# Moving one 32-byte tile: the address phase of matmul operands in a two-layer block

## The chip, the cores and the metric

The kernel runs on one core of one Trainium2 chip. The metric is device time in microseconds (us) of one launch; the median of three runs is 1803.8 us (1799.57, 1803.80 and 1804.04). A profiled execution shows every instruction of the five engines (PE is TensorE, DVE is VectorE, ACT is ScalarE, POOL is GpSimd, SP is SyncE) and its DMA packets. PE has a second row, PEld, for the loading of weights: a matmul streams one operand (the moving one, here up to 512 columns) past another that was loaded before (the stationary one, 128 columns).

## The reference, cut to what matters

Two layers act on 256 tokens of width 2048, in float32. Each layer normalizes, applies a scale and a shift that depend on a conditioning vector, widens to 4096, mixes, and projects back. Layer 0 mixes with a Fourier transform and also works on 256 context tokens; layer 1 is windowed attention over tokens and context.

```python
h = _rmsnorm(x, norm_g[i]) * (1 + scale) + shift
if kind == 0:
    y  = _fourier_branch(h, fnet_w_in[j], fnet_w_mix[j])
    yc = _fourier_branch(hc, fnet_w_in[j], fnet_w_mix[j])
elif kind == 1:
    y, yc = _attention_branch(h, hc, attn_w_in[j], attn_sink[j], rows, cols, need_ctx)
x = x + gate * (y @ w_out[i])
...
return _rmsnorm(x, final_g)
```

## The kernel before

A float32 product is made of three matmuls on a pair of halves: each operand is split into a high part (`h`, a rounded copy of type float32r) and a low part (`l`, the rest). `mm3` (L77 to L80) issues the three: `wh` with `xh` on L78, `wh` with `xl` on L79, `wl` with `xh` on L80. In a row such as `ps<-act,wh` the first name behind the arrow is the moving operand and the second the stationary one. Weights come in pieces of 1 MB through the pool `raw`, and ACT (L65) and DVE (L66) split them into tiles `wh` and `wl` of the pool `ws`, 1024 columns each.

The stages in the order of time, with the lines that the prediction names:

- Layer 0, opening and Fourier groups, to 322 us: matmuls of 256 or 260 columns.
- Layer 0, gate product and output product, 322 to 1022 us: `mm3` with 512 columns. The moving operand is a tile of the pool `act` (the activations, both parts), the stationary one a slice of `wh` or `wl`.
- Layer 1, keys and values, 1022 to 1120 us: `mm3` with 512 columns. Here the weights move, and slices of the normalized input are stationary: `h` (tokens, 16 tiles of the pool `h1`) and `h1c` (context, pool `kvp`).
- Layer 1, attention, 1160 to 1640 us: 64 heads, and between the steps of one head come units of other products as filling: queries (`mm3`, weights moving, `h` stationary), gate (L1119 with 512 columns and L1121 with 256: `h` moves, a slice of `wh` or `wl` is stationary), and the first part of the output product. Of a head itself are L1155 and L1156 (scores: `kkh` and `kkl` move, `qa` or `qb` is stationary), the softmax on ACT (L1160, L1172) and DVE (L1157, L1173), a transpose of its result `f` into `ft` by DMA (L1175), and L1190 and L1191 (16-bit products of `ft` with the values `v`).
- Layer 1, output product, to 1787 us: `mm3` with 512 columns, weights moving and slices of the gated result stationary. That result has 32 blocks `k`; `y_split` (L976) puts blocks 0 to 15 into the pool `h1` (its slots are free by then), 16 to 23 into the pool `act`, and 24 to 31 into the pool `fin`. The tiles are called `ys` in the rows, those of `act` `act`.
- The last sums, the normalization and the stores, to 1800 us.

The order of the instructions on each engine is set by the program and a scheduler that runs when the program is built. Pools take their room in the order in which they are opened, one behind the other, each tile rounded up to 32 bytes. So the byte at which a tile begins in a partition follows from all that was opened before it. The pools `raw`, `ws` and `act` are opened early. The pool `h1` of layer 1 is opened after them and began with a 32-byte tile `dsc`, which holds one scale per key-value head (written in `d_turn`, read in `emit_y` at L1140):

```python
with tc.tile_pool(name="h1", reuse_waits="tile", bufs=16) as h1p:
    hx1 = []
    v01, vs = [], []
    dsc = h1p.tile([P, 8], F32, name="dsc", bufs=1)
```

Of the kernel before, what the change touches and what calls it, by code (L numbers as in the profile page):

```python
# [10 lines left out]
F32 = mybir.dt.float32  # L11
# [6 lines left out]
P = 128  # L18
# [13 lines left out]
def tile_dit(ctx: ExitStack, tc: tile.TileContext, a: dict, out: bass.AP):  # L32
    nc = tc.nc
    V, S, PE, GP = nc.vector, nc.scalar, nc.tensor, nc.gpsimd

    const = ctx.enter_context(tc.tile_pool(name="const", bufs=1))
# [40 lines left out]
    def mm3(o, wh, wl, xh, xl, start, stop):  # L77
        PE.matmul(o, wh, xh, start=start, stop=False)  # L78
        PE.matmul(o, wh, xl, start=False, stop=False)  # L79
        return PE.matmul(o, wl, xh, start=False, stop=stop).ins  # L80
# [18 lines left out]

    ident = const.tile([P, P], F32, name="ident")  # L100
    make_identity(nc, ident)
    ones = const.tile([P, 1], F32, name="ones")
    GP.memset(ones, 1.0)
    mhalf, pow_end = const.tile([P, 4], F32, name="mhalf"), [None]
    GP.memset(mhalf, -0.5)

    def bcast_rows(r4, dst):
        o = psum()
        for t in range(4):
            PE.matmul(o[:, t * P : (t + 1) * P], r4[:, t : t + 1].broadcast_to([P, P]), ident, start=True, stop=True)  # L110
        S.copy(dst, o)
# [54 lines left out]
    with tc.tile_pool(name="st", reuse_waits="tile", bufs=1, side="right") as st:  # L166
# [3 lines left out]
        ss = st.tile([P, 4], F32, name="ss")  # L170
# [716 lines left out]
    with tc.tile_pool(name="h1", reuse_waits="tile", bufs=16) as h1p:  # L887
        hx1 = []
        v01, vs = [], []
        dsc = h1p.tile([P, 8], F32, name="dsc", bufs=1)  # L890
        kT = []
        with tc.tile_pool(name="kvp", reuse_waits="tile", bufs=2) as kvp:
            hc1 = []
# [70 lines left out]
        with tc.tile_pool(name="at", reuse_waits="tile", bufs=2) as at:  # L964
# [4 lines left out]
            def w1_next():  # L969
                n = kg1[0]  # L970
                kg1[0] += 1
                if n % 2 == 0:
                    raw1[0] = raw(a["wo1a"][n // 2])
                return half_split(raw1[0], n % 2)

            def y_split(k):  # L976
                if 16 <= k < 24:
                    t = act(F32R)
                else:
                    t = (h1p if k < 16 else fin[0]).tile([P, 512], F32R, tag="h1" if k < 16 else "ys", name="ys", bufs=16)  # L980
                split(t[:, 0:N], t[:, N : 2 * N], y1[k // 2][:, (k % 2) * N : (k % 2 + 1) * N], GP if k < 24 else V)
                yh.append(t)

            def o1_step(k, os_, wh, wl):
                while len(yh) <= min(k + 4, NB - 1) and (len(yh) < 24 or fin):
                    y_split(len(yh))
                for tb in range(2):
                    mm3(os_[tb], yh[k][:, tb * P : (tb + 1) * P], yh[k][:, N + tb * P : N + (tb + 1) * P], wh, wl, k == 0, k == NB - 1)
# [251 lines left out]
        with tc.tile_pool(name="fin", reuse_waits="tile", bufs=1) as fp:  # L1240
# [7 lines left out]
                    nc.gpsimd.dma_start(x2[tb][c], x1d[tb, :, c * 512 : (c + 1) * 512])  # L1248
            fg = fp.tile([P, D], F32, name="fg")
            nc.gpsimd.dma_start(fg, a["fg"].broadcast_to([P, D]))  # L1250
            ss = fp.tile([P, 9], F32, name="ss")

            sum_end = [None]

            def evac(tb, cb, o, c0=0, c1=512, col=None, square=True):
                col = tb * 4 + cb if col is None else col
                q, qx = slice(cb * 512 + c0, cb * 512 + c1), slice(c0, c1)
                t, x = act()[:, 0 : c1 - c0], x2[tb][cb][:, qx]
                V.tensor_tensor(t, o[:, qx], gbc[:, q], op=ALU.mult)
                sum_end[0] = V.tensor_tensor(x, x, t, op=ALU.add).ins  # L1260
                if square:
                    S.activation(t, x, AF.Square, accum_out=ss[:, col : col + 1])
                if cb < 3:
                    GP.tensor_tensor(x, x, fg[:, q], op=ALU.mult)

            for k in range(24, NB, 2):
                w = w1_next()
                for i in range(2):
                    o1_step(k + i, oA, *(t[:, i * 512 : (i + 1) * 512] for t in w))
            for tb in range(2):  # L1270
                evac(tb, 0, oA[tb])
            o = [[psum() for _ in range(2)] for _ in range(2)]
# [182 lines left out]
```

## Time and profile before

| | before |
|---|---|
| median of three runs | 1803.8 us |
| span of the profiled execution | 1799.6 us (the lowest of the three runs, 1799.57, to the digit shown) |
| PE busy | 1765.1 us, 98% |
| DVE, ACT, POOL busy | 1411.3, 898.3, 213.5 us |
| instructions | 26039 |
| granted TensorE clock, mean | 0.998 |
| transfers | 398.86 MB, mean 222 GB/s |

A row of the profile's groups has the line, the engine, the operation, the tiles and their shape, the count, the busy time in us, the mean ns of one, and behind the second bar the idle time of the engine just before them. [...]

### The profile page before, as it was taken

To read this page: it belongs to the slowest core of one execution; us is meant where nothing else is said; L and a number is where in the kernel's file an instruction comes from. 1 tells how busy PE (TensorE), PEld (TensorE's weight loads), DVE (VectorE), ACT (ScalarE), POOL (GpSimd) and SP (SyncE) were. 2 spreads that over 40 slices of the span, in tenths; PEclk is the share of its full clock that TensorE was granted. 3 is DMA by queue.
4 is the path that set the end of the run, shared out by engine and by line. 5 is a ranking of instruction groups with operands and counts; after the bars stand their busy time and mean duration, and the time that the engine had idled before them with its cause. 6 is when DMAs were issued, how large, how long until landed. Compare 5 with 4: busy or idle time off the path is not lost. (4 is left out here: it accounts for less than half of the span.)

```text
span 1799.6 us, 26039 instructions
## 1 busy us (share of the span) xinstructions
PE 1765.1 (98%) x9449; PEld 1478.0 (82%) x9449; DVE 1411.3 (78%) x2761; ACT 898.3 (50%) x1543; POOL 213.5 (12%) x213
## 2 busy tenths in 40 slices
PE   6999999999999999999999999999999999999998
PEld 4679999888888888888888888878888788887886
DVE  5779888786978888775976563989999899997455
ACT  5545445432222242323322443678887788886343
POOL 0001112100000000000001000332212212233001
PEclk9999999999999999999999999999999999999999
DMA  9998889666666757663558322488888988888553
GB/s 393 417 341 230 236 228 249 230 227 241 239 229 234 260 194 264 245 223 117 189 203 336 120 104 94 168 189 217 213 209 204 211 209 209 211 211 263 192 176 140
DMA packets 205248, 398.86 MB, mean 222 GB/s; under 512 B 152064, under 2 KB 152464, under 8 KB 170048
## 3 DMA queue, kind: packets, MB, share of 16 engines
q1 hardware_dynamic: 181056, 359.19, 61.7%
q0 software_dynamic: 19920, 31.06, 6.7%
q10 hardware_dynamic: 4144, 6.95, 1.2%
q8 instruction: 74, 1.21, 0.3%
q14 instruction: 54, 0.44, 0.1%
HBM read 352.06 MB, written 12.59 MB: 203 GB/s over the span
## 5 line engine op out<-in xcount | busy, mean ns | idle before, releaser
L65 ACT CAST wh<-raw 128x1024 fp32r<-128x1024 f32 x333 | 348.3, 1048 | 532.4 <-PE ps L79 431.6
L66 DVE TENSOR_TENSOR wl<-raw,wh 128x1024 fp32r<-128x1024 f32 x333 | 428.0, 1289 | 219.1 <-ACT wh L65 215.4
L79 PE MATMUL ps<-act,wh 128*128 128x512 f32 x1024 | 398.2, 389 | 0.0
L78 PE MATMUL ps<-act,wh 128*128 128x512 f32 x1024 | 393.7, 389 | 0.0
L80 PE MATMUL ps<-act,wl 128*128 128x512 f32 x1024 | 392.8, 389 | 0.0
L80 PEld LDWEIGHTS ps<-act,wl 128*128 128x128 f32 x1024 | 192.2, 188 | 39.9
L79 PEld LDWEIGHTS ps<-act,wh 128*128 128x128 f32 x1024 | 192.2, 188 | 39.8
L78 PEld LDWEIGHTS ps<-act,wh 128*128 128x128 f32 x1024 | 192.2, 188 | 39.7
L1119 PE MATMUL ps<-h,wh 128*128 128x512 f32 x512 | 184.8, 396 | 0.0
L686 DVE CUSTOM_DVE_ANT_0 raw<-raw,cb 128x512 f32<-128x512 f32 x256 | 172.7, 689 | 12.7 <-DMA raw<-in_adw 8.9
L686 DVE CUSTOM_DVE_ANT_0 junk<-raw,cb 128x512 f32<-128x512 f32 x192 | 132.1, 688 | 31.0 <-DMA raw<-in_adw 20.4
L1121 PE MATMUL ps<-h,wl 128*128 128x256 f32 x512 | 138.6, 281 | 0.0
L79 PE MATMUL ps<-wl,h 128*128 128x512 f32 x320 | 126.9, 397 | 0.3 <-DVE wl L66 0.3
L80 PE MATMUL ps<-wh,h 128*128 128x512 f32 x320 | 125.3, 395 | 0.0
L78 PE MATMUL ps<-wh,h 128*128 128x512 f32 x320 | 124.0, 402 | 0.0
L1173 DVE SCALAR_TENSOR_TENSOR f<-p,sm,f 128x512 f16<-128x512 f32 x128 | 105.6, 844 | 11.1 <-ACT f L1172 10.9
L1119 PEld LDWEIGHTS ps<-h,wh 128*128 128x128 f32 x512 | 96.2, 188 | 18.9
L1160 ACT ACTIVATE p<-ps,mx 128x512 f32<-128x512 f32 x128 | 88.0, 689 | 36.9 <-DVE mx L1157 30.8
L1172 ACT ACTIVATE f<-p,sm 128x512 f16<-128x512 f32 x128 | 87.6, 717 | 33.6 <-DMA ft<-f 15.5
L1121 PEld LDWEIGHTS ps<-h,wl 128*128 128x128 f32 x512 | 96.6, 189 | 2.8
L1157 DVE CUSTOM_DVE_ANT_0 ps<-ps,mask,nsink 128x512 f32<-128x512 f32 x128 | 93.5, 750 | 0.9 <-PE ps L1156 0.7
L79 PE MATMUL ps<-wl,ys 128*128 128x512 f32 (+1 forms) x192 | 75.2, 392 | 0.0
(339 smaller groups left out, 3379.3 us busy)
## 6 DMA issues: line engine op xcount, KB each, us to landing
raw<-in_wz SPq DMA_DIRECT2D x64, 1024.0 KB, 5.4
raw<-in_adw SPq DMA_DIRECT2D x64, 1024.0 KB, 5.2
raw<-in_awp SPq DMA_DIRECT2D x32, 1024.0 KB, 13.0
raw<-in_wo SPq DMA_DIRECT2D x32, 1024.0 KB, 5.5
raw<-in_wq SPq DMA_DIRECT2D x32, 1024.0 KB, 5.3
raw<-in_wu SPq DMA_DIRECT2D x32, 1016.0 KB, 6.1
raw<-in_wo1b SPq DMA_DIRECT2D x16, 1024.0 KB, 4.9
act<-in_xT POOLq DMA_DIRECT2D x32, 256.0 KB, 6.0
```

What stands on the lines that cost most here:

```text
L65: last_cast[0] = S.copy(h, src).ins
L66: last_sub[0] = eng.tensor_tensor(l, src, h.bitcast(F32), op=ALU.subtract).ins
L78: PE.matmul(o, wh, xh, start=start, stop=False)
L79: PE.matmul(o, wh, xl, start=False, stop=False)
L80: return PE.matmul(o, wl, xh, start=False, stop=stop).ins
L686: V.tensor_tensor_reduce(junk if s == 0 and i < 3 else wf, wf, cb[:, s, kq * 512 : kq * 512 + 512], 1.0, 0.0, ALU.mult, ALU.add, acc[:, i, ...
L1119: PE.matmul(o[0], wh[:, q], hx1[k], start=k == 0, stop=k == KT - 1)
L1121: PE.matmul(o[0][:, 0:N], wl[:, q], hx1[k][:, 0:N], start=False, stop=False)
L1157: V.tensor_tensor_reduce(o, o, mask[:, tb, :], -0.125, nsink[:, i : i + 1], ALU.add, ALU.min, mx[:, tb : tb + 1])
L1160: S.activation(pt[tb], so[tb], AF.Exp, bias=mx[:, tb : tb + 1], scale=-1.0, accum_out=sm[:, tb : tb + 1])
L1172: S.activation(f[:, 0:512], pt[tb], AF.Copy, scale=sm[:, tb : tb + 1])
L1173: V.scalar_tensor_tensor(f[:, 512:1024], pt[tb], sm[:, tb : tb + 1], f[:, 0:512], op0=ALU.mult, op1=ALU.subtract)
```

## The change

The two constants `ones` (4 bytes in a partition) and `mhalf` (16 bytes) each took 32 bytes of the pool `const`. They become slices of one tile `consts` of 32 bytes: columns 0 to 3 hold -0.5, columns 4 to 7 hold 1.0. In the 32 bytes so freed stands `dsc`, which leaves the pool `h1`. The pool `const` keeps its length, so nothing that is opened between the two moves; all that is opened from `h1` on begins 32 bytes lower. Besides, the 36-byte tile `ss` of the last stage is taken after blocks 24 to 31 of `ys` in the pool `fin` and not before them.

```diff
@@ constants
-    ones = const.tile([P, 1], F32, name="ones")
-    GP.memset(ones, 1.0)
-    mhalf, pow_end = const.tile([P, 4], F32, name="mhalf"), [None]
+    consts = const.tile([P, 8], F32, name="consts")
+    ones, mhalf, pow_end = consts[:, 4:5], consts[:, 0:4], [None]
+    GP.memset(consts[:, 4:8], 1.0)
     GP.memset(mhalf, -0.5)
+    dsc = const.tile([P, 8], F32, name="dsc")
@@ layer 1
     with tc.tile_pool(name="h1", reuse_waits="tile", bufs=16) as h1p:
         hx1 = []
         v01, vs = [], []
-        dsc = h1p.tile([P, 8], F32, name="dsc", bufs=1)
         kT = []
@@ last stage
             nc.gpsimd.dma_start(fg, a["fg"].broadcast_to([P, D]))
-            ss = fp.tile([P, 9], F32, name="ss")
-
             sum_end = [None]
...
                 for i in range(2):
                     o1_step(k + i, oA, *(t[:, i * 512 : (i + 1) * 512] for t in w))
+            ss = fp.tile([P, 9], F32, name="ss")
             for tb in range(2):
                 evac(tb, 0, oA[tb])
```

In the built program the instructions of every engine stand in the same order as before, with the same shapes and the same waits; only start addresses differ. The start of a tile in its partition, modulo 256 bytes (slices of 128 float32 columns keep it, being 512 bytes apart):

| tiles | role in layer 1 | before | now |
|---|---|---|---|
| `wh`, `wl`, `act`, `v` (pools `ws`, `act`) | moving, stationary | 224 | 224 |
| `h` (and `ys`, blocks 0 to 15) | stationary, moving | 0 | 224 |
| `h1c` | stationary | 0 | 224 |
| `kkh`, `kkl` | moving | 0 | 224 |
| `qa`, `qb` | stationary | 0 | 224 |
| `ys`, blocks 24 to 31 | stationary | 64 | 224 |
| `p`, `gbc`, `fg` | not of a matmul | 0 | 224 |
| `f`, `ft` (in and out of the DMA transposes; `ft` moves in L1190, L1191) | moving | 192 | 160 |

The tiles `raw`, `ws` and `act` lie in the lower part of a partition (bytes 19,680 to 136,416), those that the change shifts above it (from byte 142,048 on). In layer 0's Fourier groups, whose tiles don't move, some operands of 256 and 260 columns stay at other values than 224.

## The prediction

> **What bounds the kernel now.** I read the page first, then the busy times by stage, then the chain of waits with the matmuls' starts.
>
> ```profile
> span 1799.6 us, 26039 instructions
> PE 1765.1 (98%) x9449; PEld 1478.0 (82%) x9449; DVE 1411.3 (78%) x2761; ACT 898.3 (50%) x1543; POOL 213.5 (12%) x213
> ```
>
> PE is busy all the time; the question is whether it is the bound in layer 1, the only part whose addresses move. The table of stretches (columns: stretch, time, then busy time and count of PE, PEld, DVE, ACT, POOL, the granted clock, the DMA engines' share, GB/s) answers:
>
> ```profile
> 400.00:800.00 400.00, 400.00 (x1767) 331.20 (x1766) 325.26 (x766) 114.28 (x137) 5.88 (x11) 1.00 0.65 238
> 1040.00:1100.00 60.00, 60.00 (x259) 48.31 (x258) 30.42 (x54) 19.25 (x31) 0.00 (x0) 1.00 0.27 95
> 1022.00:1120.00 98.00, 97.81 (x447) 79.69 (x447) 52.18 (x99) 41.95 (x72) 1.58 (x2) 1.00 0.34 119
> 1172.00:1600.00 428.00, 423.92 (x2346) 353.39 (x2347) 398.74 (x738) 348.30 (x689) 100.65 (x73) 1.00 0.86 208
> 1650.00:1787.00 137.00, 137.00 (x592) 110.90 (x591) 73.87 (x74) 55.41 (x67) 12.61 (x8) 1.00 0.50 175
> ```
>
> In keys and values and in the output product PE has no gap, and the next engine (DVE) is busy 53% and 54%: there a nanosecond less for a matmul is a nanosecond of the end. In attention PE is busy 99%, but DVE 93% (398.74 of 428) and the DMA engines 86%: PE still sets the pace, with little room before another does. The clock is granted in full throughout.
>
> What does a 512-column matmul cost? 400 to 800 us (layer 0, both operands at 224) holds 1767, of which some two reach over the edges: 400.0/1765 = 226.6 ns from start to start. 1040 to 1100 us (layer 1, weights at 224 moving, `h` or `h1c` at 0 stationary): 60.0/257 = 233.5 ns. Same clock, same shape, no gap: 6.9 ns more. The chain of waits shows it best, in one stage with one line of code and the same moving tiles (columns: start, duration, what; one row per block `k`, which is 4 times the three matmuls of `mm3`):
>
> ```profile
> 1657.08 0.93 PE ps L78 x4
> ...
> 1699.08 0.93 PE ps L78 x4
> ...
> 1701.88 0.91 PE ps L78 x4
> 1704.60 0.91 PE ps L78 x4
> 1707.32 0.91 PE ps L78 x4
> ...
> 1720.92 0.91 PE ps L78 x4
> 1723.64 0.94 PE ps L78 x4
> ...
> 1726.45 0.94 PE ps L78 x4
> ...
> 1729.26 0.94 PE ps L78 x4
> ```
>
> Blocks 0 to 15 (`ys` at 0): 16 steps from 1657.08 to 1701.88, 2.80 us each, 233.3 ns a matmul. Blocks 16 to 23 (the same data in `act`, at 224): 8 steps to 1723.64, 2.72 us, 226.7 ns. Block 24 on (`ys` at 64): 5.62 us for two, 234.2 ns. Nothing but the place of the stationary operand changes at these two borders. The groups say the same by duration (mean ns behind the busy time):
>
> ```profile
> L79 PE MATMUL ps<-act,wh 128*128 128x512 f32 x1024 | 398.2, 389 | 0.0
> L79 PE MATMUL ps<-wl,h 128*128 128x512 f32 x320 | 126.9, 397 | 0.3 <-DVE wl L66 0.3
> L79 PE MATMUL ps<-wl,ys 128*128 128x512 f32 x184 | 73.0, 397 | 0.0
> L79 PE MATMUL ps<-wl,act 128*128 128x512 f32 x56 | 21.8, 390 | 0.0
> ```
>
> **The change, part by part.** It removes and adds no instruction and no wait; two memsets of `ones` and `mhalf` become two of one tile, at the start. All that can act is where operands begin. I take it that equal phase (224 for both) costs 226.7 ns wherever the tile lies.
>
> (a) Matmuls with 512 columns, weights moving. By the three lines of `mm3`: `h` 3 × 320 = 960, `h1c` 3 × 64 = 192, `ys` 3 × 184 = 552, and 12 with both moving `act` and stationary `ys`: 1716. At 2.80 − 2.72 us over 12 matmuls, 6.67 ns each: 11.4 us. Of them 3 × 192 = 576 lie between 1172 and 1600 us: 3.8 us in attention, 7.6 us outside.
>
> (b) The scores, where both operands stand at 0, and (c) the gate's pair L1119 and L1121. The timeline of PE:
>
> ```profile
> 1501.02 0.40 PE L1155 MATMUL ps<-kkh,qa 128*128 128x512 f32 x1
> 1501.26 0.39 PE L1156 MATMUL ps<-kkl,qa 128*128 128x512 f32 x1
> 1501.48 0.39 PE L1155 MATMUL ps<-kkh,qa 128*128 128x512 f32 x1
> 1501.71 0.40 PE L1156 MATMUL ps<-kkl,qa 128*128 128x512 f32 x1
> 1501.95 0.40 PE L1119 MATMUL ps<-h,wh 128*128 128x512 f32 x1
> ...
> 1502.30 0.39 PE L1119 MATMUL ps<-h,wh 128*128 128x512 f32 x1
> 1502.53 0.28 PE L1121 MATMUL ps<-h,wl 128*128 128x256 f32 x1
> ...
> 1504.38 0.39 PE L1119 MATMUL ps<-h,wh 128*128 128x512 f32 x1
> ```
>
> Four score matmuls take 0.93 us, 232.5 ns each, though both stand at 0; but inside (0.24, 0.22, 0.23, 0.24) the slow steps are those at the border to another product, and the step from `kkl` to the next `kkh` takes 0.22. So equal phase is quick here too, in the upper part of the partition, and the border costs. At 226.7 ns: 5.8 × 256 = 1.5 us; bounds 0 and that. The gate's pairs: six in 2.08 us, 0.347 each, about 0.23 for the 512 columns (`h` at 0 moving) and 0.12 for the 256. I put 3 ns on the first and nothing on the second, since the 256-column row shows no quicker kind: 3 × 512 = 1.5 us. Bounds: nothing, and the whole pair by the ratio 2.72/2.80, 10 ns × 512 = 5.1 us.
>
> (d) L1190 and L1191: `ft` stood at 192 against `v` at 224 and now stands at 160. Unequal before and after, so nothing; if the 2.9% of (a) were lost or won on two times 256 matmuls of about 0.11 us, 1.6 us either way:
>
> ```profile
> 1497.46 0.27 PE L1191 MATMUL ps<-ft,v 128*128 128x256 f16 x1
> 1497.57 0.27 PE L1190 MATMUL ps<-ft,v 128*128 128x256 f16 x1
> 1497.68 0.27 PE L1191 MATMUL ps<-ft,v 128*128 128x256 f16 x1
> ```
>
> (e) The other engines write and read shifted tiles too. The same cast into `ys` (0 and 64) and into `act` (224) costs the same, so nothing:
>
> ```profile
> L65 ACT CAST ys<-act 128x256 fp32r<-128x256 f32 x24 | 8.2, 403 | 0.7 <-DVE act L1140 0.7
> L65 ACT CAST act<-act 128x256 fp32r<-128x256 f32 x8 | 2.6, 399 | 0.0
> ```
>
> Sum: 7.6 outside attention, and 3.8 + 1.5 + 1.5 = 6.8 in attention. There the saving comes back in part: 6.8 us off 428 brings DVE from 93% to 95%, and what is late next is the softmax's chain, on which PE waits already.
>
> ```profile
> PE ps L1190 <- DMA ft<-f: 4.7, 4, 2.1
> ```
>
> That row of the waits (us in total, times, longest) shows a reserve that runs out 4 times in some 60 heads. I keep three quarters, 5.1 us. Total 12.7 us: 1799.6 − 12.7 = 1786.9 for an execution like the profiled one. That execution stood 4.2 us below the median of the runs shown, 1803.8, so the median I forecast is 1791.
>
> [...]
>
> **The rivals.** [...]
>
> Second, *attention gives all of its 6.8 us back* to DVE and the softmax's chain: 7.6 remain, 1796. For it: DVE 93%. Against it: PE at 423.92 of 428 with few and short waits.
>
> Third, *slower: the DMA transposes at 160*. `f` and `ft` were at a multiple of 64 bytes and no longer are. The tile's rows from 1172 to 1600 us:
>
> ```profile
> L1175 SPq DMA_TRANSPOSE ft<-f x114: 1231/1252/5062, 1173.8 to 1593.1; - x114
> DMA to landing us min/median/max: 3.0/5.0/7.8
> ```
>
> Landing takes 5.0 us in the median; PE waits only near the longest, 7.8, so the reserve is some 2 us, spread over the two heads (428/57 = 7.5 us each) that lie between softmax and use. It decides from about 2 us more. At 3 us more, the missing 1 us over two heads is 0.5 us for each of 62 transposed heads, 31 us: 1803.8 − 7.6 + 31 = 1827. For it: DMA engines at 86%. Against it: no row shows a transfer that its phase makes slow, and `raw`, at 224, fills without PE waiting in layer 1.
>
> **How the numbers follow.** The forecast (8 to 18 us off) gets 0.64, the second rival 0.08, no change 0.20, slower 0.08. The likeliest range is 1786 (all of attention and the gate's upper bound: 12.7 + 1.7 + 3.6 = 18 off) to 1797. To hold 8 in 10 it reaches into "no change": 1785 to 1803. About 0.3%, 5.4 us, is what a measurement of this kernel tells from none: faster by more 0.72, within 0.20, slower by more 0.08.
>
> **What would show it.** Right: in the chain, the blocks 0 to 15 and 24 to 31 of the last output product step by 2.72 us; 1040 to 1100 us holds some 267 matmuls; rows `ps<-wl,h` and `ps<-wl,ys` have 389 or 390 ns, as `ps<-wl,act`. The stretch from 1650 to 1787 us gets 3 us shorter, keys and values 2.5. Wrong on place or phase: the 2.80 stays with `ys` at 224. Wrong on attention: (a) comes in, but the waits of L1190 grow by as much as PE saves. Wrong on the transposes: landing above 7 us in the median. Layer 0 must keep its 226.7 ns and its length.

## The result and the profile after

| | before | after |
|---|---|---|
| median | 1803.8 us (7 runs, 1799.57 to 1804.44) | 1796.89 us (7 runs, 1792.52 to 1799.28) |
| ratio, 95% interval | | 0.9962 [0.9951, 0.9973] |
| span of the profiled execution | 1799.6 us | 1794.8 us |

The kernel is 0.38% faster: 6.9 us by the medians, 4.8 us by the two profiled executions. The profiled execution of before is the fastest of its seven and that of after lies near its median, so the two profiles show less of the gain than the medians do. The forecast of 1791 us had the sign right and the result lies in its range, but about half of the gain is missing. The page's first lines, after:

```profile
span 1794.8 us, 26039 instructions
PE 1759.0 (98%) x9449; PEld 1478.9 (82%) x9449; DVE 1410.7 (79%) x2761; ACT 899.5 (50%) x1543; POOL 211.5 (12%) x213
```

The table of stretches answers to the one in the prediction (stretch, time, busy time and count of PE, PEld, DVE, ACT, POOL, granted clock, share of the DMA engines, GB/s):

```profile
400.00:800.00 400.00, 400.00 (x1766) 331.20 (x1766) 325.20 (x766) 114.11 (x137) 5.89 (x11) 1.00 0.65 238
1040.00:1100.00 60.00, 60.00 (x267) 49.69 (x266) 29.89 (x54) 19.88 (x31) 0.00 (x0) 1.00 0.26 92
1172.00:1600.00 428.00, 425.41 (x2356) 354.56 (x2356) 396.12 (x740) 350.49 (x694) 99.58 (x76) 1.00 0.86 208
1650.00:1787.00 137.00, 135.77 (x610) 112.43 (x608) 76.70 (x81) 55.88 (x70) 12.78 (x8) 1.00 0.50 176
```

Layer 0 does the same work in its stretch (1766 matmuls, 1767 before). Keys and values hold 267 matmuls in 60 us, 259 before: 60.0/265 = 226.4 ns each, layer 0's price. The chain of waits in the last output product (start, duration, what; one row per block of 12 matmuls):

```profile
1657.49 0.91 PE ps L78 x4
...
1698.29 0.91 PE ps L78 x4
1701.01 0.91 PE ps L78 x4
...
1720.05 0.91 PE ps L78 x4
...
1728.21 0.91 PE ps L78 x4
```

Every step is 2.72 us, through both borders at which it changed before: 15 steps from 1657.49 to 1698.29 are 40.80 us, 10 from 1701.01 to 1728.21 are 27.20. The groups (mean ns behind the busy time) show the same, and one row that went the other way:

```profile
L79 PE MATMUL ps<-wl,h 128*128 128x512 f32 x320 | 125.1, 391 | 0.5 <-DVE wl L66 0.5
L79 PE MATMUL ps<-wl,ys 128*128 128x512 f32 x184 | 71.8, 390 | 0.1
L79 PE MATMUL ps<-wl,act 128*128 128x512 f32 x56 | 21.8, 390 | 0.0
L1119 PE MATMUL ps<-h,wh 128*128 128x512 f32 x512 | 187.1, 403 | 0.0
```

The gate's wide matmul, L1119, was quicker in the kernel before:

```profile
L1119 PE MATMUL ps<-h,wh 128*128 128x512 f32 x512 | 184.8, 396 | 0.0
```

Its timeline shows it from start to start (a matmul of 512 columns lasts 0.39 us there and the next one starts 0.23 us after it: neighbours overlap). Before (start, duration, engine, line, tiles), four pairs in 1.39 us:

```profile
1299.98 0.39 PE L1119 MATMUL ps<-h,wh 128*128 128x512 f32 x1
1300.21 0.28 PE L1121 MATMUL ps<-h,wl 128*128 128x256 f32 x1
...
1301.37 0.39 PE L1119 MATMUL ps<-h,wh 128*128 128x512 f32 x1
```

and after, four pairs in 1.41 us:

```profile
1300.01 0.40 PE L1119 MATMUL ps<-h,wh 128*128 128x512 f32 x1
1300.24 0.28 PE L1121 MATMUL ps<-h,wl 128*128 128x256 f32 x1
...
1301.42 0.40 PE L1119 MATMUL ps<-h,wh 128*128 128x512 f32 x1
```

**Where the time went.** From the starts of all matmuls in the trace, layer 1 can be cut into four stages: from the first matmul on keys and values to the last, to the first score, to the last product with `v`, to the last matmul of the program.

| stage, us | before | after | difference |
|---|---|---|---|
| keys and values | 89.45 | 86.94 | −2.5 |
| to the first score | 42.21 | 41.29 | −0.9 |
| attention, first score to last product with `v` | 480.85 | 482.61 | +1.8 |
| rest of the output product | 149.43 | 146.57 | −2.9 |

Outside attention 6.3 us came in (the remaining 0.3 us of the 4.8 lie before layer 1). Attention kept none of its share: it grew by 1.8 us, of which 1.7 are a drop of the clock that this execution has and that of before has not (below). The same starts, grouped by kind, give the mean distance to the next matmul, with longer steps (over 250 ns behind 512 columns, over 130 behind 256) counted as one plain step and the rest apart, as idle time:

| matmuls of layer 1, from start to start | before, ns | after, ns | difference in all |
|---|---|---|---|
| `h` in `mm3`, 960 | 233.4 | 228.4 | −4.8 us |
| `h1c`, 192 | 233.3 | 226.7 | −1.3 us |
| `ys`, 587 (some with 256 columns) | 229.1 | 222.9 | −3.6 us |
| scores, 256 | 230.9 | 229.0 | −0.5 us |
| gate L1119, 512 | 230.4 | 235.3 | +2.5 us |
| gate L1121, 512 | 118.1 | 117.2 | −0.5 us |
| L1190 and L1191, 512 | 100.6 | 100.8 | +0.1 us |

`h` fell from 233.3 to 226.9 ns in keys and values, but only from 233.5 to 229.0 in attention. Together TensorE's own work is 8.1 us shorter. The last matmul starts 4.8 us earlier (1790.4 to 1785.6 us), and the idle time in layer 1 has grown from 17.0 to 20.4 us. So two things need a cause: the gate, and 3.4 us of idle time. The waits of PE from 1172 to 1655 us (us in total, times, longest), before:

```profile
PE ps L1190 <- DMA ft<-f: 4.7, 4, 2.1
PE ps L1190 <- ACT f L1172: 1.1, 2, 0.7
PE ps L1190 <- DVE ft L1183: 0.9, 1, 0.9
```

and after:

```profile
PE ps L1190 <- DMA ft<-f: 1.8, 2, 1.0
PE ps L1190 <- DVE ft L1183: 1.7, 1, 1.7
PE ps L1182 <- DVE f L1173: 1.0, 1, 1.0
```

The drop of the clock at the start of attention that this execution has (0.70, 0.50 and 0.95 in the slices of 2 us from 1168 to 1174 us, 1.00 in before; at 0.50 the scores step by 0.42 to 0.43 us, in before by 0.23) counts 1.7 us in those 20.4, half of the growth; the run e2 below has none, and 20.0 us of idle time all the same.

The waits in the middle shrank; what grew is idle time in the last heads. The stretch 1620 to 1640 us, before:

```profile
1620.00:1640.00 20.00, 18.95 (x118) 14.79 (x116) 18.06 (x34) 17.48 (x34) 11.46 (x15) 1.00 0.83 228
```

and after, with PE busy 2.6 us less:

```profile
1620.00:1640.00 20.00, 16.31 (x110) 12.69 (x109) 16.82 (x25) 14.61 (x30) 12.38 (x18) 1.00 0.86 271
```

The chain that ended last, in the stretch 1570 to 1650 us, by line; before:

```profile
by line: PE ps L1119 18.0%; PE ps L80 12.8%; PE ps L78 12.5%; PE ps L79 12.2%; PE ps L1121 9.4%; PE ps L1190 5.3%; PE ps L1191 4.9%; PE ps L1155 4.1%; PE ps L1156 4.0%; issue 3.6%; ACT wh L65 3.2%; ACT act L65 3.0%; ACT f L1172 1.9%; ACT p 
```

and after:

```profile
by line: DVE wl L66 14.3%; issue 11.5%; DVE f L1173 10.9%; DMA ft<-f 10.2%; PE ps L78 6.9%; PE ps L80 6.9%; DVE ps L1157 6.9%; PE ps L79 6.6%; ACT wh L65 4.9%; ACT p L1160 4.0%; DVE ob L1197 3.4%; ACT ys L65 2.1%; DVE th L1128 1.9%; ACT f L
```

Before, this end was a chain of matmuls; after, it is VectorE's splits and softmax with their transposes. That gave the theory for the second question: VectorE's work sets when attention ends, and TensorE's savings turn into idle time there. The experiments speak for the first half and leave the second open.

### The profile page after: what moved, and what is told of

It is laid out like the page before. It is cut to its first block, busy times and chain, and to the rows that moved or that the text cites. A ratio compares the mean times of both kernels' runs of the same rounds, so it can differ in the third digit from the quotient of the medians.

```text
span 1794.8 us, 26039 instructions
## 1 busy us (share of the span) xinstructions
PE 1759.0 (98%) x9449; PEld 1478.9 (82%) x9449; DVE 1410.7 (79%) x2761; ACT 899.5 (50%) x1543; POOL 211.5 (12%) x213
## 5 line engine op out<-in xcount | busy, mean ns | idle before, releaser
L1119 PE MATMUL ps<-h,wh 128*128 128x512 f32 x512 | 187.1, 403 | 0.0
L1121 PE MATMUL ps<-h,wl 128*128 128x256 f32 x512 | 138.4, 281 | 0.0
L1119 PEld LDWEIGHTS ps<-h,wh 128*128 128x128 f32 x512 | 96.5, 188 | 20.7
L1121 PEld LDWEIGHTS ps<-h,wl 128*128 128x128 f32 x512 | 96.9, 189 | 3.0
## 6 DMA issues: line engine op xcount, KB each, us to landing
raw<-in_awp SPq DMA_DIRECT2D x32, 1024.0 KB, 12.7
```

What stands on the lines that cost most here:

```text
L1119: PE.matmul(o[0], wh[:, q], hx1[k], start=k == 0, stop=k == KT - 1)
L1121: PE.matmul(o[0][:, 0:N], wl[:, q], hx1[k][:, 0:N], start=False, stop=False)
```

## The experiments

Those with a ratio were timed in several rounds beside the kernel before; e3, e4, e7 and e8 ran once each. In e1 to e8 and e12 the whole computation is done.

### Is it the phase, the value, or the place?

e2 adds 32 bytes to the constants, so that `ws`, `act` and all that layer 1 shifts stand at 0; e3 and e4 put layer 1's upper tiles at 128 and 192 and leave `ws` and `act` at 224.

```diff
@@ e2
+    const.tile([P, 8], F32, name="pad")
@@ e3 (40 columns) and e4 (56)
-        gr = const.tile([KT, P], F32, name="gr")
+        gr = act()[0:KT, 0:P]
...
+    l1c.tile([P, 40], F32, name="pad")
```

> The changed kernel with 32 bytes more in the constants: raw, ws, act and all tiles of layer 1 that the change moved begin at 0 modulo 256 and not at 224, moving and stationary operands still in equal phase. Nothing is left out. If it is the difference of the two phases that counts: 227 ns for the 512-column matmuls of layer 0 and of layer 1's queries, keys, values and output product, and the time of the changed kernel, 1797 us within 3. If the value 224 counts: layer 0's 3072 matmuls go from 227 to 233 ns, 18 us more, and layer 1's some 1700 too, 11 us more: some 1825 us.

> The changed kernel with layer 1's pools 160 bytes higher (room from a 512-byte constant that goes to the activations' pool): h, h1c, ys, kkh, qa at 128, weights at 224. Nothing is left out. If any unequal phase costs the same: mm3 of layer 1 at 233 to 234 ns, as at 0 and 64; the gate's L1119 near 230, as at 0. If the cost follows the distance of the phases: another number, for mm3 between 227 and 240.

> As the one before, with layer 1's tiles at 192: 32 bytes below the weights, where the kernel before has them 32 above (0 against 224). If the sign does not count: mm3 at 233 ns, L1119 at 230. [...]

e2: 1795.91 us, ratio 0.9962 [0.9948, 0.9976], as after; `h` 228.3 ns, `h1c` 226.7, gate 235.0; attention 482.05 us, and PE busy 15.84 us of 1620 to 1640. e3: 1802.34 us, `h1c` 233.4, `h` 233.8, gate 230.1. e4: 1801.30 us, `h1c` 233.3, `h` 233.6, gate 234.3. The stretch in keys and values, for e2:

```profile
1040.00:1100.00 60.00, 60.00 (x267) 49.67 (x266) 29.75 (x53) 20.00 (x31) 0.00 (x0) 1.00 0.25 88
```

and for e3:

```profile
1040.00:1100.00 60.00, 60.00 (x258) 48.27 (x258) 30.05 (x54) 18.86 (x30) 0.00 (x0) 1.00 0.26 91
```

So neither the value 224 nor the place in the partition counts, but that weights and `h` stand at the same phase. Each unequal value tried (before −32, e3 +96, e4 +32, as weights minus `h`) costs the same 6.6 ns on `h1c`. All of these, and the +160 of `ys` at 64, are odd multiples of 32 bytes: for `mm3` these runs don't tell a period of 256 bytes from one of 64. The gate answers otherwise: it is dearest at equal phase (235 ns), nearly as dear at +32 (234.3) and cheap at +96 and −32 (230.1, 230.4); as +32 and +96 differ, its period is not 64.

### The gate alone

e1 keeps equal phase and lets the gate issue its eight wide matmuls in a row, then its eight narrow ones (in the second half the other way round):

```diff
-                    for k in range(i * 8, i * 8 + 8):
-                        q = slice((k % 8) * P, (k % 8 + 1) * P)
-                        for part in (0, 1) if k < KT - 1 else (1, 0):
+                    for part in (0, 1) if i == 0 else (1, 0):
+                        for k in range(i * 8, i * 8 + 8):
+                            q = slice((k % 8) * P, (k % 8 + 1) * P)
```

> The changed kernel, with the gate's matmuls of half a unit in two groups: first the eight of 512 columns (L1119), then the eight of 256 (L1121), and the other way round in the second half, instead of in turns. Nothing is left out. In the changed kernel a pair costs 235 + 117 = 352 ns, before it 230 + 118 = 348. [...] Theory B (a tile at 224 that moves is slow as such): L1119 stays at 235, time as the changed kernel, 1797.

L1119 fell from 235.3 to 228.3 ns and L1121 rose from 117.2 to 119.2, 2.6 us less for the gate; but 1814.41 us, ratio 1.0061 [1.0048, 1.0073], with attention at 500.7 us (6.8 of them lost to drops of the clock). The build put the work of VectorE, ScalarE and the transposes in another order too, and the waits of PE in attention show where it hurts:

```profile
PE ps L1190 <- DMA ft<-f: 12.4, 12, 4.9
```

It tells that equal phase is dear for the gate only where a wide and a narrow matmul alternate; of attention's length it tells nothing, since the order changed with it.

e5 to e8 move the gate's weights alone: `wh` and `wl` of the gate begin `c` columns into a longer tile (c = 0, 24, 32, 56: +0, +96, +128 and −32 bytes against `h`, modulo 256). To make room, `gr` goes to `act`, `th` has 2 buffers and `ob` 3; e5, at +0, is the control for that. Its order differs from that of after in the last heads (52 matmuls stand elsewhere, from 1606 us on), and e6 to e8 have its order.

```diff
-    def half_split(t, i):
-        h = wsp.tile([P, 1024], F32R, tag="ws", name="wh")
-        l = wsp.tile([P, 1024], F32R, tag="ws", name="wl")
+    def half_split(t, i, c=0):
+        h = wsp.tile([P, 1088], F32R, tag="ws", name="wh")[:, c : c + 1024]
+        l = wsp.tile([P, 1088], F32R, tag="ws", name="wl")[:, c : c + 1024]
...
-                return half_split(raws1[src], i % 2)
+                return half_split(raws1[src], i % 2, 24 if kind == "z" else 0)
```

> A control for the next three: the changed kernel with the slots of ws widened from 4096 to 4352 bytes (room from the constant gr, a buffer of th and a buffer of ob), all phases as in the changed kernel, the gate's weights at 224 too. Nothing is left out. L1119 at 235 ns, L1121 at 117; time as the changed kernel, 1797 us, or a few us more if one buffer less of th or ob makes somebody wait.

> The control with the gate's weight tiles alone (wh and wl of the gate) 96 bytes further on in their slots, at 64 modulo 256, while h stays at 224; all other weights stay at 224. Order and waits are the control's. If the phase between h and the gate's weights is what made L1119 slower: 230 ns as in the run at phase 128 (weights 96 above h there too), 512 times 5 ns, 2.6 us below the control, with mm3 still at 226.7. If L1119 at 235 is due to where h moves from, or to other engines: no change, 235.

> As the one before with the gate's weights 128 bytes further on, at 96 modulo 256. A distance that no run has shown for the gate: if only equal and plus 32 are bad, 230 ns; if the cost falls with distance up to half of 256, less, 227.

> As the one before with the gate's weights at 192, 32 below h, the distance of the kernel before (224 against 0): if the distance alone counts, L1119 and L1121 go back to the 230.4 and 118.1 ns of the kernel before.

| | e5, +0 | e6, +96 | e7, +128 | e8, −32 |
|---|---|---|---|---|
| gate L1119, ns | 235.3 | 230.4 | 232.2 | 230.4 |
| gate L1121, ns | 117.2 | 117.6 | 119.0 | 118.1 |
| attention, us | 483.78 | 484.92 | 485.01 | 483.90 |
| time, us | 1798.44 | 1798.36 | 1799.23 | 1797.93 |

e5 has ratio 0.9970 [0.9958, 0.9982], e6 0.9974 [0.9964, 0.9984]. `h1c` stays at 226.7 ns in all four, so the gate's price follows its own weights' phase. e8, at the distance of the kernel before, returns to that kernel's 230.4 and 118.1 ns, as expected; e7 meets neither of the values put for it (230 or 227). But the 2.3 us that e6 saves on L1119 and L1121 do not show in the time: 1798.36 against 1798.44 us. The scores take 0.4 us of them back (229.1 to 230.6 ns). Part of the rest stands in the clock. The stretch of the last heads in e8, in slices of 2 us:

```profile
1624.00:1626.00 2.00, 0.04 (x1) 0.07 (x2) 2.00 (x3) 1.98 (x6) 1.91 (x2) 1.00 0.96 225
1626.00:1628.00 2.00, 2.00 (x16) 1.85 (x17) 2.00 (x6) 1.94 (x6) 2.00 (x4) 0.69 0.89 369
1628.00:1630.00 2.00, 2.00 (x6) 1.52 (x6) 1.69 (x5) 0.40 (x2) 2.00 (x5) 0.50 0.53 111
1630.00:1632.00 2.00, 2.00 (x11) 1.46 (x9) 0.00 (x0) 0.63 (x1) 1.85 (x4) 0.96 0.85 299
```

VectorE works through (2.00 us busy), PE waits, and soon after PE goes on, the granted clock falls to 0.50: 6 matmuls fit into 2 us, not 11. Over these slices (0.31 + 0.50 + 0.04) × 2 = 1.7 us of full speed are lost. e7 loses 1.7 us there too, e6 3.4 (its profiled execution, 1800.54 us, was the longest of its ten; 2.0 of the 3.4 lie before the last product with `v`), e5 nothing. Less these, attention is 483.8 us in e5 and 483.0, 483.3 and 482.2 in e6, e7 and e8: 0.8, 0.5 and 1.6 us less, where the gate saves 2.3, 0.7 and 2.0. This is an estimate, since it takes for granted that nothing else would have waited there, and the differences are of the size of that between after and e2, which have one order and all phases equal (480.9 us without the drop, 482.05). So it isn't shown that the saving reached the last heads. Nor is it shown that it made PE's gap there longer: the longest is 2.83 us in e8, 2.69 in e6 and 2.29 in e7, each with a drop of the clock behind it, but 2.31 in e5 without one. How often an execution without a profile meets such a drop isn't seen.

### Does VectorE hold attention?

e9, e10 and e11 are before, after and e6 with two of VectorE's operations on the gate left out, 64 in all; the instructions of e9 and e10 stand in the same order (which isn't that of before and after).

```diff
                         S.copy(zs, o[0][:, N : 2 * N])
-                        V.tensor_tensor(zs, o[0][:, 0:N], zs, op=ALU.add)
                         S.activation(th, zs, AF.Tanh, scale=0.5)
-                        V.scalar_tensor_tensor(th, th, 1.0, zs, op0=ALU.add, op1=ALU.mult)
```

> The kernel before, without the two VectorE operations of the gate's silu (the sum into zs and the product into th are left out, so y is not gated with silu; ScalarE's copy and tanh stay). That takes 64 operations of 412 and 436 ns, 27 us, off VectorE in attention and nothing off TensorE. Theory (VectorE's softmax chain sets when attention ends, so TensorE's savings there are not seen): attention, 480.9 us from the first score to the last product with v, gets shorter by 3 us or more, and the whole run with it, 1800 us or less. Rival (attention is held by its DMA traffic or by the fixed order of TensorE's own work): attention stays within 1 us of 480.9.

> The kernel after with the same two operations left out (y is not gated with silu); its instructions stand in the same order as those of the eased kernel before. Theory: TensorE now sets attention in both, so what attention gave back is seen again: products with h and act 5 to 6.5 ns cheaper (3.8 us), scores 0.5 us cheaper, gate 2.5 us dearer, so attention is 1 to 2.5 us shorter than the eased kernel before's, instead of 1.8 longer, and the whole difference is 7.3 to 8.8 us. Rival: attention is as long or 1 to 2 us longer than in the eased kernel before, and the whole difference is 4.5 to 6.3 us.

> The kernel with the gate's weights at +96 bytes to h, all else as after, and the same two operations left out (y is not gated with silu). Theory: with VectorE out of the way the gate's 2.5 us count as well, so attention is 3.5 to 5 us shorter than the eased kernel before's and about 2.5 us shorter than the eased kernel after's. Rival: no shorter than the eased kernel after's. Its order differs in some places from the other two, which can blur a microsecond.

| | before | after | e9 | e10 | e11 |
|---|---|---|---|---|---|
| time, us | 1803.8 | 1796.89 | 1801.40 | 1793.10 | 1789.17 |
| ratio to before | 1 | 0.9962 | 0.9996 [0.9985, 1.0007] | 0.9942 [0.9927, 0.9957] | 0.9918 [0.9900, 0.9936] |
| span profiled, us | 1799.6 | 1794.8 | 1798.7 | 1790.9 | 1787.2 |
| attention, us | 480.85 | 482.61 | 480.06 | 478.60 | 475.09 |
| idle of PE in layer 1, us | 17.0 | 20.4 | 16.2 | 16.6 | 15.2 |
| lost to the clock in attention, us | 0 | 1.7 | 1.7 | 1.7 | 1.7 |
| attention without that, us | 480.9 | 480.9 | 478.4 | 476.9 | 473.4 |

Two parts of the expectation have to be kept apart. Between e9 and e10, which differ only in addresses and both have the drop, attention is 1.5 us shorter (1 to 2.5 expected) where before and after are equal without the drop. The idle time grows by 0.4 us where it grew by 3.4 (1.7 without the drop), and the times differ by 8.3 us (7.3 to 8.8 expected), the whole of TensorE's saving (8.1 us between before and after). And the cheap gate now counts: e11 stands 3.9 us under e10, attention 3.5 us (2.5 expected; the extra microsecond may come from its somewhat other order). In none of the three does the clock drop in the last heads; each has one drop of 1.7 us at the start of attention, 1168 to 1176 us, as after has.

For the kernel before the test decides nothing. As measured, attention of e9 is 0.8 us shorter than that of before, where the theory asked for 3 and its rival for less than 1; without the drop, which before's execution doesn't have, it is 2.5 us shorter. The times leave room for both: the interval of e9's ratio reaches from 2.7 us faster to 1.3 us slower.

The executions with the whole computation tell more. TensorE's own work in attention (the plain steps, as above) is 2.6 us more in e4 than in before, 0.2 more in e3, 1.5 less in after and 1.7 less in e2, all in one order of instructions; attention, without the lost clock, is 481.0, 482.2, 480.9 and 482.1 us, and 480.9 in before. So it does not follow TensorE's work either way. In e9, e10 and e11 that work is 0, 1.6 and 3.7 us less than in before, and attention goes with it: 478.4, 476.9 and 473.4 us. These are single executions each, with a scatter of about 1 us.

The chain that ended last, 1570 to 1650 us, in e10 (lines two lower than in after):

```profile
by line: PE ps L1119 13.8%; PE ps L80 12.8%; PE ps L78 12.2%; PE ps L79 12.2%; PE ps L1121 7.1%; issue 5.2%; PE ps L1188 4.9%; PE ps L1189 4.4%; DVE f L1171 3.8%; DVE wl L66 3.4%; PE ps L1153 2.9%; PE ps L1154 2.8%; DVE ps L1155 2.8%; ACT w
```

Matmuls again. So in the whole kernel the length of attention looks to be set by something other than TensorE's work, and with less work on VectorE it goes with TensorE's work again. In the last heads PE waits for VectorE's chain (before against e2, with no drop of the clock in the attention of either: 3.1 us less of PE's work in 1620 to 1640). That TensorE's savings open this wait is not shown: e3, whose matmuls cost what those of before cost, has two waits there as long as those of after (PE's waits from 1172 to 1655 us, lines one higher):

```profile
PE ps L1191 <- DVE ft L1184: 1.7, 1, 1.7
PE ps L1183 <- DVE f L1174: 1.0, 1, 1.0
```

And behind some of PE's gaps of 2.0 us and more the granted clock is 0.50 for a while, at the start of attention (after, e1, e5 to e11) and in the last heads (e6 to e8); e1 has two more such drops, around 1580 and 1643 us, and e12 one, around 1576 us. What these runs don't separate is VectorE's load from the order of its work in the last heads, since the eased pair has both less work and another order than before and after.

### The whole computation with less on VectorE

e12 is e6 with the silu's product on GpSimd:

```diff
-                        V.scalar_tensor_tensor(th, th, 1.0, zs, op0=ALU.add, op1=ALU.mult)
+                        nc.gpsimd.tensor_tensor(th, th, zs, op=ALU.mult)
+                        nc.gpsimd.tensor_tensor(th, th, zs, op=ALU.add)
```

> The complete computation: gate weights at +96 bytes as in the run of that name, and the silu's product th = (1 + th) zs computed by GpSimd in two operations (th zs, then + zs), 14 us less for VectorE. Theory: attention falls below the 484.9 us of the run with the gate at +96 alone, by 2 to 6 us, and the total comes to 1792 to 1796 us, a version that beats both kernels. Rival: GpSimd's two operations come late for y, or the other order that the scheduler makes of it costs more than VectorE's 14 us bring: 1797 us or more.

1807.51 us, ratio 1.0023 [1.0013, 1.0033]: slower than before, attention 493.7 us. The rival held. The waits of PE from 1172 to 1655 us:

```profile
PE ps L1191 <- DMA ft<-f: 14.9, 15, 3.2
```

The build ordered the engines' work anew here as well, and two of VectorE's other operations got dearer: `f` 882 ns where after has 821, the sum `sm` 349 where it has 225 (groups from 1172 to 1600 us). The split `wl`, which reads two tiles (`raw` and `wh`) where `sm` reads `sm` and `es`, hardly did (1333 ns, 1328 in after). So the cause of these two rows stays open. How much of the 9 us more than e6 is order and how much those operations wasn't separated. No kernel with the whole computation beat the kernel after beyond the intervals; e2 equals it.

## Why the prediction was right, and where it missed

- **What bounds the kernel.** Right for the stages with PE at 100%: keys and values and the output product took every nanosecond, 2.5 and 2.9 us where 2.5 and 3 had been named. For attention "PE still sets the pace, with little room before another does" is not borne out: in e4 TensorE has 2.6 us more to do there than in before, and attention is as long (481.0 and 480.9 us).
- **(a) Equal phase costs 226.7 ns anywhere.** Right: 226.7 on `h1c`, 2.72 us for each block at the formerly slow addresses, and unequal again slow (233.3 to 233.8) at two other values. That the period is 256 bytes is not shown. The sum was 11.4 us and came to 9.7, because `h` in attention, among other products, stays at 229.0. Outside attention 7.6 was summed and 6.3 came. Before the first score it was 0.9 us in place of 1.3: of the 192 matmuls summed there 161 lie before it, and they gave 5.4 ns each, not 6.67. In the rest of the output product it was 2.9 in place of 3.8: 96 of the `ys` matmuls run before the last product with `v`, which is 0.6 us, and the idle time behind it is 0.3 us longer.
- **(b) The scores.** 1.5 us forecast, 0.5 measured (230.9 to 229.0 ns), within the bounds of 0 and 1.5. Most of the border's cost stayed.
- **(c) The gate.** The failing term of the sum: −1.5 us forecast with bounds of 0 and 5.1, and +2.0 measured (+2.5 on L1119, −0.5 on L1121). The step that failed is "equal phase costs 226.7 ns wherever the tile lies": it was read from rows of 512 columns in a row and carried to a product of 512 beside 256, for which no row of the trace stood at equal phase. A bound below nothing was missing; nothing excluded it.
- **(d), (e)** `ft` at 160: 100.8 ns against 100.6, as put. Casts into `ys` 404 ns, 403 before.
- **Three quarters of attention's saving kept.** Wrong: none was kept. Nor was there 6.8 us to keep from: TensorE's own work in attention fell by 1.5 us. In the sum's own terms 12.7 us was forecast and the profiled execution gave 4.8. Of the 7.9 missing, the matmuls account for 6.3 (14.4 us of savings summed, 8.1 measured), and idle time for the rest (1.7 us of give-back forecast, as 14.4 less 12.7, and 3.4 us measured, 1.7 of it the drop of the clock that only after's execution met). By the medians 6.9 of the 8.1 us came in. The mechanism was named (VectorE's softmax chain is late next), and the row that warned was VectorE's 398.74 of 428 us; its price was guessed from the few waits before, which say how much reserve is used up, not how much is left.
- **The rivals.** The second, "attention gives all of its 6.8 us back, 1796", has the number that came, 1796.89, and it got 0.08. In part that is luck: attention did keep nothing, but it had 1.5 us to give back and not 6.8, and outside it 6.3 us came and not 7.6. No change, which had 0.20, did not come: the reading that the place of a tile counts and not its phase fell at the first stretch. 226.7 against 233.3 ns with nothing but addresses changed says that for these float32r matmuls addresses do count; by what means isn't seen. The transposes at 160 did not get slower: landing fell from 5.0 to 4.8 us in the median.

```profile
L1175 SPq DMA_TRANSPOSE ft<-f x114: 1231/1250/5042, 1171.2 to 1598.4; - x114
DMA to landing us min/median/max: 3.0/4.8/7.8
```

## What to carry to other kernels

Where a stage has one engine at 99% and another at 93%, busy shares don't tell what a saving on the first is worth: here VectorE had some 29 of 428 us free, and 1.5 us less for TensorE brought nothing. Ease the second engine in an experiment before a gain on the first is counted, and read the granted clock behind each gap before two executions are compared: one drop of 1.7 us was as large as the difference in question. A price read from one pattern of instructions (wide matmuls in a row) holds for that pattern; for another (wide and narrow in turn) both signs belong in the bounds until a row shows it. And if operands' addresses can be chosen, an address adds no instruction (26039 before and after), but try it for each product apart.

## What was not expected of the hardware

- Matmuls of 512 float32r columns took 226.7 ns from start to start (`h1c`) when both operands began at the same phase modulo 256 bytes (224 and 224 in after, 0 and 0 in e2), and 233.3 to 233.4 at each unequal distance tried (weights minus `h` of −32 in before, +32 in e4, +96 bytes in e3). No distance of 64 or 128 bytes was tried for them.
- For 512 and 256 columns in turn, with the roles exchanged (`h` moving, weights stationary), it was the other way: the wide one took 235.0 to 235.3 ns at 0 (e2, after, e5), 234.3 at +32 (e4), 232.2 at +128 (e7) and 230.1 to 230.4 at +96 and −32 (e3, e6, before, e8); grouped by eight at 0 it took 228.3 (e1). What makes one distance dearer than another stays open: no run tells it.
- Around gaps of 2 us and more in PE's work the granted clock fell to 0.50 in some executions. Each drop seen in layer 1 cost 1.7 us (as 3.4 us at 0.50 would) or twice that: after gaps of 2.29, 2.69 and 2.83 us in e7, e6 and e8, but not after 2.31 us in e5. All fourteen profiled executions have a gap of 2.0 to 2.2 us at the start of attention; behind it the clock drops in nine (after, e1, e5 to e11) and not in five (before, e2, e3, e4, e12). So gaps of equal length had unequal ends, and the length alone does not decide; what does isn't shown. In e1 and e12 a drop began while PE still stood idle (clock 0.65 from 1640 to 1642 us in e1, 0.93 from 1572 to 1574 us in e12, with 0.00 us of PE in both).
